# Storing weight differences ahead: the first difference pinned on VectorE, its load two units earlier

## The chip, the cores and the metric

One core of a Trainium2 chip runs the whole kernel. TensorE (PE) multiplies, with its weight loads (PEld) beside it; ACT (ScalarE) and DVE (VectorE) do element-wise work; POOL (GpSimd) here issues the stores and small copies; SP (SyncE) issues the loads. The metric is the device time of one execution in microseconds. The kernel before took 1654.93 us (median of 3 runs, 1653.99 to 1656.75).

## The reference

One decoder layer on 256 tokens of width 2048, in float32:

```
proj = x @ w_in                     # GLA q,k,v,gate,low-rank; FoX q,k,v,forget; two merge gates
o    = gla_chunked(q, k, v, log_a)  # 4 heads, then RMSNorm and swish gate
of   = fox_attention(...)           # 8 heads, causal softmax with forget bias
mix  = (sigmoid(ma)*(o @ w_branch_gla) + sigmoid(mb)*(of @ w_branch_fox)) @ w_out
x    = layer_norm(ALPHA*x + mix)
g    = causal_dwconv(x @ w_gate, conv_w, conv_b)
x    = layer_norm(ALPHA*x + (gelu(g) * (x @ w_up)) @ w_down)
x    = x + sigmoid(x @ w_ple_gate) * (p @ w_ple_proj)
```

Nearly all the work is the products of 256 tokens with large weight matrices, each weight read once.

## The kernel before

**Units.** The weights come in 284 units of 128 x 2048 floats (1 MB), in the order in which they are used (`wu`). Each is loaded by SP in two halves into `raw` (a ring of five buffers). To keep float32 accuracy each half is split: ACT rounds it to `hi` (L120), DVE subtracts to get `lo` (L233), and PE multiplies with both (L299, L301). `hi` and `lo` have six buffers each, three units. `unit()` hands out the next unit and first prepares those up to three ahead, so loads and splits run ahead of PE.

**Stages.** After a start with the FoX values (to about 51 us) come FoX q/k (16 units), GLA q/k (16), the first twenty merge gates, GLA values and gate (32), the other merge gates, the branch projections (24), the output projection (16), gate and up of the MLP (88), down (44) and the last gate (16). Each unit of the first stages ends in an eviction of its PSUM bank: ACT copies half into `tmp`, DVE adds (`comb`, L320 to L330). Small work is woven in by generators: `mixers` (FoX attention and others) and `levels` (the masks and decays of GLA, whose DVE steps `e`, `kq`, `at` alternate with small PE products `pa`).

**Strassen units and stored units.** Some units of the GLA value and gate, output, down and last stages are multiplied by Strassen's scheme in seven products; their four blocks of 512 columns have to be replaced by four differences. Most such units do this when they are prepared. Thirty-one of them do it long before, in stages where there is room ("parked" in the code): `park_gen` loads the unit into a buffer of the S8 pool (`td`), DVE makes the four differences in place (`differences`, L155 to L163, the subtraction on L158), POOL stores the result to a DRAM tensor (L174), and `prep_s` later loads it back (L188). Fifteen of them belong to the GLA value and gate stages and are stored during FoX q/k, GLA q/k and the first merge gates; five belong to the output projection and are stored during the branch projections; eleven belong to down and are stored during gate and up. `park_gen` is a generator: one pull issues the load, the next the four differences and the store.

**The S8 pool** has fifteen buffers of 8 KB a partition. Activations (`xT`, `x1T`, four each), `gq`, `gk`, `gb`, `kq`, `at`, the merge gates `sg`, the hidden activations `hC` (ten of them by the end of gate and up) and the stored units all live there. A load into it waits until the buffer's last user is done.

**What sets the order.** SP's queue is in program order (`manual_schedule`): a load that waits holds back all loads behind it. The other engines' instructions are put in order when the program is built, by a planner with its own costs and the program order as priority; on the chip each engine then goes through its list in that order. `tc.keep_in_program_order(i)` forbids the planner to place an instruction ahead of the one traced just before it on the same engine.

Of the kernel before, what the change touches and what calls it, by code (L numbers as in the profile page):

```python
# [19 lines left out]
P = 128  # L20
# [3 lines left out]
NF = DFF // P  # L24
# [53 lines left out]
def tile_block(ctx: ExitStack, tc: tile.TileContext, wu, wfv, wpp, xT_in, x_in, pT_in, wlr,  # L78
               chan, gnorm, lng, ident_in, mask_in, cmask_in, out):
    nc = tc.nc  # L80
# [23 lines left out]
    def s8(shape, dt=F32, name=None):  # L104
        return big.tile(shape, dt, tag="S8", name=name)

    def t1(name):
        return sm.tile([P, 256], F32, tag="t1", bufs=6, name=name)
# [20 lines left out]
    for _ in range(8):  # L129
# [5 lines left out]
    dn0 = NU - 16 - NF  # L135
# [7 lines left out]
    parked = {b + nh * len(order[nh]) + order[nh].index(n): None  # L143
              for b, order, tset in ((52, GV_ORDER, GV_T), (68, GV_ORDER, GR_T), (120, OUT_ORDER, WO_T),
                                     (dn0, DN_ORDER, DN_T))
              for nh in range(2) for n in tset[nh]}
    parked = {u: i for i, u in enumerate(sorted(parked))}
    td = dr.tile([len(parked), P, 2048], F32, name="td")
# [4 lines left out]
        o = 0 if any(u in r for r in UA) else LO_SHIFT  # L153
        return rlo.tile([P, 1152], F32R, tag="lo", name=f"lo{name}")[:, o:o + 1024]

    def differences(r0, r1, h):
        b12, b11, b22, b21 = r0[:, 0:512], r0[:, 512:1024], r1[:, 0:512], r1[:, 512:1024]
        sub = lambda o, a, b: nc.vector.tensor_tensor(o, a, b, ALU.subtract)  # L158
        if h == 0:
            sub(b11, b12, b11)  # L160
            sub(b12, b12, b22)
        else:
            sub(b22, b22, b11)  # L163
            sub(b21, b21, b22)

    def park_gen(units):

        for u, i in [(u, i) for u, i in parked.items() if u in units]:
            w = s8([P, 2048], name=f"td{i}")
            nc.sync.dma_start(w, wu[u])  # L170
            yield
            for h in range(2):
                differences(w[:, 0:1024], w[:, 1024:2048], h)
            nc.gpsimd.dma_start(td[i], w)  # L174
            yield

    def prep_s(u):

# [33 lines left out]
        if u not in parked:  # L212
            differences(r0, r1, 0)
        t3, t1_ = split(rt[0], "t13")
        if u not in parked:
            differences(r0, r1, 1)
# [24 lines left out]
    def unit(ahead=3):  # L241
        u = n_used[0]
        n_used[0] += 1
        while n_prep[0] < min(NU, u + ahead):
            prep()
        return ready.pop(u)
# [36 lines left out]
    def load_consts2():  # L283
        nc.sync.dma_start(gnb, gnorm.broadcast_to([P, 512]))
        for i in range(2):
            maskf = ring.tile([P, 4, 256], F32, tag="raw", bufs=5, name=f"maskf{i}")
            nc.sync.dma_start(maskf, mask_in[:, 8 * i:8 * i + 8, :].rearrange(
                "p (l t) n -> p l (t n)", t=2))
            nc.gpsimd.tensor_copy(mask[:, 4 * i:4 * i + 4, :], maskf)


    def w_unit(ps, hi, lo, act, kts, first, last, hoff=0, tick=None):


        n = len(kts)
        for i, kt in enumerate(kts):
            a = act[kt // 4]
            w0 = (hoff + i) * P
            nc.tensor.matmul(ps, lhsT=hi[i // 8 if hoff == 0 else 0][:, w0 % 1024:w0 % 1024 + P],  # L299
                             rhs=a[:, kt % 4, :], start=first and i == 0, stop=False)  # L300
            nc.tensor.matmul(ps[:, 256:512],  # L301
                             lhsT=lo[i // 8 if hoff == 0 else 0][:, w0 % 1024:w0 % 1024 + P],
                             rhs=a[:, kt % 4, 0:256], start=False, stop=last and i == n - 1)
            if tick is not None:
                tick(i)
# [15 lines left out]
    def comb(ps, o, scale=1.0):  # L321
        tmp = t1("tmp")
        copy(tmp, ps[:, 256:512], scale)
        a = ps[:, 0:256]
        if len(o.shape) == 3:
            a, tmp = [v.rearrange("p (t n) -> p t n", t=2) for v in (a, tmp)]
        if scale == 1.0:
            nc.vector.tensor_tensor(o, a, tmp, ALU.add)
        else:
            nc.vector.scalar_tensor_tensor(o, a, scale, tmp, ALU.mult, ALU.add)  # L330
# [19 lines left out]
    def pull(n, gens=mixers):  # L350
        for _ in range(n):
            while gens:
                try:
                    next(gens[0])
                    break
                except StopIteration:
                    gens.pop(0)
# [92 lines left out]
    for u in range(8):  # L450
        hi, lo = fvu[u]
        for j in range(2):
# [8 lines left out]
            for t, i, c in seq:  # L461
                o, n = fch[c]
                w, x = prods[t][i]
# [34 lines left out]
    for t in range(2):  # L498
        for c, (o, n) in enumerate(fch):
            n = min(n, 1024 - o)  # L500
# [136 lines left out]


    fqk = {}
    parks = [park_gen(range(52, 84))]  # L640
    load_consts2()
    mixers.append(fox_gen())
    for n in range(16):
        h, j = n // 2, n % 2
        hi, lo = unit()

        ps = (mxtile if n == 0 else mmtile)(f"psf{'qk'[j]}{h}")
        w_unit(ps, hi, lo, xT, range(16), True, True,
               tick=lambda i: pull(1) if i == 7 else None)
        if n % 8 == 0:  # L650
            fqk[h // 4] = s8([P, 4, 2, 256], name=f"fqk{h // 4}")
        comb(ps, fqk[h // 4][:, h % 4, j], (P ** -0.5, 1.0)[j])
        if 8 <= n < 15:
            pull(1, parks)
    tc.keep_in_program_order(nc.scalar.preload_act_table_set("exp_and_others"))

# [10 lines left out]
    def a_gen():  # L667
# [70 lines left out]
        for h in range(H):  # L738
# [8 lines left out]
            for lev in (1, 3, 5, 7):  # L747
                level_put(h, lev)
                if lev < 7:
# [2 lines left out]
                    level(h, lev + 3)  # L752
                    yield

    gq, gk = [s8([P, H, 512], name=n) for n in ("gq", "gk")]
    levels.append(a_gen())


    for n in range(16):
        nm, dst, sc = (("q", gq, 1.0 / 16.0), ("k", gk, 1.0))[n // 2 % 2]  # L760
        h, c = n // 4, n % 2
# [145 lines left out]
    def x_sums(pairs):  # L907
        for i, pair in pairs:
            if i == 0:
                o = s8([P, 8, 256], F32R, name="xS")  # L910
            if i < 2:
                ws = [o[:, 4 * i:4 * i + 4, :]]
            elif i == 3:
                w = ec.tile([P, 2, 512], F32R, tag="vh", name="xS3")
                ws = [w.rearrange("p j (i n) -> p (j i) n", i=2)]
            else:
                ws = [sm.tile([P, 2, 256], F32R, tag="t2", bufs=6, name=f"xS{i}{j}")
                      for j in range(2 if i == 2 else 1)]
                if i == 4:
                    w = ec.tile([P, 512], F32R, tag="vl", name="xS4")  # L920
                    ws.append(w.rearrange("p (i n) -> p i n", i=2))
            m = 4 // len(ws)
            xS[pair] = [ws[j // m][:, j % m, :] for j in range(4)]
            y = t2("xy").rearrange("p (k t) -> p k t", t=S)
            nc.sync.dma_start(y, xT_in[:, 2 * pair:2 * pair + 2, :])
            v = s_sums(y)
            for j, w in enumerate(ws):
                src = v[:, j * m:j * m + m]
                copy(w[:, :, 0:P], src)
                nc.vector.tensor_tensor(w[:, :, P:256], src, w[:, :, 0:P].bitcast(F32),  # L930
                                        ALU.subtract)
            yield
# [15 lines left out]
    def merge_gate(n, tick=None):  # L948
        hi, lo = unit()
        ps = mmtile(f"psm{n}")  # L950
        w_unit(ps, hi, lo, xT, range(16), True, True, tick=tick)
        if n % 8 == 0:
            sg[n // 8] = s8([P, 8, 256], name=f"sg{n // 8}")
        dst = sg[n // 8][:, n % 8, :]
        comb(ps, dst)
        nc.scalar.activation(dst, dst, AF.Tanh, bias=0.0, scale=0.5)

    for n in range(PSM1):
        if 3 <= n < 18:
            pull(1, parks)  # L960
        if n == PSM1 - 6:
            mixers.append(x_sums(list(enumerate(X_S))[:3]))

        merge_gate(n, lambda i: pull(1, levels) if (16 * n + i) * 25 // (16 * PSM1)
                   != (16 * n + i + 1) * 25 // (16 * PSM1) else None)
        pull(1)
# [109 lines left out]
    for n in range(PSM1, 32):  # L1076
        if n in (26, 28):
            i = n // 2 - 13
# [8 lines left out]

    mC, mS = {}, {}
    fhl = None
    parks = [park_gen(range(120, 136))]  # L1090
    for n in range(16):
        hi, lo = unit()
        psa = mmtile(f"psa{n}")
# [25 lines left out]
        i = WO_C.index(pair)  # L1119
# [228 lines left out]
    tc.keep_in_program_order(nc.scalar.preload_act_table_set("gelu_apprx_tanh_and_others"))  # L1348
    late.tile([P, GAPS[2]], F32, name="gap2")
    hC = {}  # L1350
    parks = [park_gen(range(dn0, dn0 + NF))]
    n0 = 6

    def gate_up(name):
# [7 lines left out]
    for n in range(NF):  # L1362
# [18 lines left out]
        u = t1("up")  # L1381
# [4 lines left out]
        if pair in DN_S[0]:  # L1386
            if j == 0:
                yp = t2("yp").rearrange("p (k t) -> p k t", t=S)
            h = yp[:, j, :]
        else:  # L1390
            h = y
# [4 lines left out]
        if pair in DN_S[0] and j == 1:  # L1396
            v = s_sums(yp)
            for i in range(2):
                w = sm.tile([P, 2, 256], F32R, tag="t2", bufs=6, name="hs")
# [291 lines left out]
```

## Time and profile before

| | us |
|---|---|
| median of 3 runs | 1654.93 |
| the profiled execution | 1654.67 |
| its span, first to last instruction | 1652.9 |
| PE busy | 1644.5 |
| PE weight loads busy | 1427.2 |
| DVE busy | 1349.4 |
| ACT busy | 916.5 |

The granted clock was 0.999 of full speed over the span. Busy shares are averages over stages with different limits; a wait counts only if PE in the end waits too. A row of instructions in order of time gives start, duration, engine, line, operation, tile written and tiles read, count, and in brackets how long the engine was idle before it and who released it.

### The profile page before, as it was taken

The numbers are of one execution on the slowest core, as the hardware profiler recorded it, in microseconds if no ns is written. First come the engines' busy times: TensorE is split into PE (matmuls) and PEld (weight loads), VectorE is DVE, ScalarE is ACT, GpSimd is POOL, SyncE is SP. The second block draws the span as 40 slices with busy tenths as digits, with TensorE's granted clock in tenths as the row PEclk, the third lists the DMA queues.
The fourth block names the chain that finished last, engine by engine and source line by source line (L and its number), as shares of the span: only waits on it lengthen the run. The fifth ranks groups of instructions, "written<-read, shape, count | busy, mean of one in ns | idle before, by whom it ended". The sixth has DMA issues, their size and how long they took to land.

```text
span 1652.9 us, 24378 instructions
## 1 busy us (share of the span) xinstructions
PE 1644.5 (99%) x8851; PEld 1427.2 (86%) x8851; DVE 1349.4 (82%) x1988; ACT 916.5 (55%) x1332; POOL 83.1 (5%) x232
## 2 busy tenths in 40 slices
PE   9999999999999999999999999999999999999998
PEld 9988888888888888888898888888888888888887
DVE  7668878998888767978987887787877788988887
ACT  6645545656656654545575455455554556556553
POOL 0000000000000000000010101111101000000000
PEclk9999999999999999999999999999999999999999
DMA  9769688978877657878856787777776779899564
GB/s 323 255 207 357 209 299 292 349 280 304 300 276 268 208 199 273 295 256 295 306 179 203 273 311 254 259 268 273 253 275 239 266 265 339 305 336 337 183 226 127
DMA packets 109512, 442.99 MB, mean 268 GB/s; under 512 B 12440, under 2 KB 13728, under 8 KB 94416
## 3 DMA queue, kind: packets, MB, share of 16 engines
q1 hardware_dynamic: 101616, 395.29, 68.6%
q0 software_dynamic: 7776, 46.15, 7.4%
q8 instruction: 69, 1.13, 0.3%
q14 instruction: 51, 0.42, 0.1%
HBM read 395.24 MB, written 46.15 MB: 267 GB/s over the span
## 4 chain that ended last, share of the span: by engine, by line
PE 92%; DVE 4%; DMA 3%; ACT 1%; issue 1%; SPq 0%; POOL 0%; ACTq 0%; DVEq 0%; POOLq 0%
PE psu L299 10%; PE psg L299 9%; PE dn L830 9%; PE psm L299 5%; PE psu L301 5%; PE psg L301 5%; PE wo L830 4%; PE psa L299 4%; PE gr L830 3%; PE gv L830 3%; PE dn_p L830 3%; PE psm L301 3%; PE pg L345 3%; PE fv L464 2%; PE psa L301 2%; PE psfk L299 2%
## 5 line engine op out<-in xcount | busy, mean ns | idle before, releaser
L233 DVE TENSOR_TENSOR lo<-raw,hi 128x1024 fp32r<-128x1024 f32 x470 | 569.4, 1219 | 133.4 <-ACT hi L120 131.3
L120 ACT ACTIVATE hi<-raw 128x1024 fp32r<-128x1024 f32 x470 | 492.7, 1057 | 309.2 <-issue 109.6
L299 PE MATMUL psu<-x1T,hi 128*128 128x512 f32 x688 | 240.5, 392 | 0.0
L299 PE MATMUL psg<-x1T,hi 128*128 128x512 f32 x672 | 234.9, 392 | 0.0
L301 PE MATMUL psu<-x1T,lo 128*128 128x256 f32 x688 | 192.4, 280 | 0.0
L301 PE MATMUL psg<-x1T,lo 128*128 128x256 f32 x672 | 187.9, 280 | 0.0
L299 PE MATMUL psm<-xT,hi 128*128 128x512 f32 x512 | 180.0, 395 | 0.0
L299 PEld LDWEIGHTS psu<-x1T,hi 128*128 128x128 f32 x688 | 129.2, 188 | 27.6
L299 PEld LDWEIGHTS psg<-x1T,hi 128*128 128x128 f32 x672 | 126.2, 188 | 26.9
L301 PE MATMUL psm<-xT,lo 128*128 128x256 f32 x512 | 143.3, 280 | 0.0
L301 PEld LDWEIGHTS psu<-x1T,lo 128*128 128x128 f32 x688 | 130.6, 190 | 0.0
L301 PEld LDWEIGHTS psg<-x1T,lo 128*128 128x128 f32 x672 | 127.6, 190 | 0.0
L120 ACT ACTIVATE hi_b<-raw 128x512 fp32r<-128x512 f32 x98 | 81.8, 841 | 72.1 <-DMA raw<-in_wu_dram 26.0
L207 DVE TENSOR_TENSOR lo_b<-raw,hi_b 128x512 fp32r<-128x512 f32 x98 | 92.7, 953 | 31.3 <-ACT hi_b L120 31.2
L158 DVE TENSOR_TENSOR td<-td 128x512 f32<-128x512 f32 x124 | 84.9, 684 | 37.4 <-DMA td<-in_wu_dram 36.6
L299 PEld LDWEIGHTS psm<-xT,hi 128*128 128x128 f32 x512 | 96.2, 188 | 20.0
L830 PE MATMUL dn<-hi,hC 128*128 128x512 f32 x352 | 98.0, 389 | 0.0
L301 PEld LDWEIGHTS psm<-xT,lo 128*128 128x128 f32 x512 | 97.2, 190 | 0.2
L299 PE MATMUL psa<-oT,hi 128*128 128x512 f32 x256 | 89.5, 392 | 0.0
L830 PEld LDWEIGHTS dn<-hi,hC 128*128 128x128 f32 x352 | 66.0, 188 | 13.7
L207 DVE TENSOR_TENSOR lo_t<-td,hi_t 128x1024 fp32r<-128x1024 f32 x62 | 73.3, 1218 | 5.0 <-ACT hi_t L120 4.2
L120 ACT ACTIVATE hi_t<-td 128x1024 fp32r<-128x1024 f32 x62 | 64.2, 1054 | 15.8 <-DMA td<-td 10.7
(406 smaller groups left out, 3259.5 us busy)
## 6 DMA issues: line engine op xcount, KB each, us to landing
raw<-in_wu_dram SPq DMA_DIRECT2D x537, 512.0 KB, 5.7
td<-in_wu_dram SPq DMA_DIRECT2D x31, 1024.0 KB, 8.5
td<-td POOLq DMA_DIRECT2D x31, 1024.0 KB, 7.2
td<-td SPq DMA_DIRECT2D x31, 1024.0 KB, 7.7
hS<-sd SPq DMA_DIRECT2D x11, 1024.0 KB, 8.4
raw<-in_wu_dram SPq DMA_DIRECT2D x31, 256.0 KB, 7.2
fvraw<-in_wfv_dram SPq DMA_DIRECT2D x13, 524.0 KB, 7.0
sd<-hs POOLq DMA_DIRECT2D x24, 256.0 KB, 6.2
```

The costliest lines, as they stand in the source:

```text
L120: return nc.scalar.activation(o, i, AF.Copy, bias=0.0, scale=scale)
L158: sub = lambda o, a, b: nc.vector.tensor_tensor(o, a, b, ALU.subtract)
L207: nc.vector.tensor_tensor(lo, src, hi.bitcast(F32), ALU.subtract)
L233: i = nc.vector.tensor_tensor(lo, raw, hi.bitcast(F32), ALU.subtract)
L299: nc.tensor.matmul(ps, lhsT=hi[i // 8 if hoff == 0 else 0][:, w0 % 1024:w0 % 1024 + P], rhs=a[:, kt % 4, :], start=first and i == 0, stop= ...
L301: nc.tensor.matmul(ps[:, 256:512], lhsT=lo[i // 8 if hoff == 0 else 0][:, w0 % 1024:w0 % 1024 + P], rhs=a[:, kt % 4, 0:256], start=False, ...
L345: nc.tensor.matmul(bs[j][:, 0:m], lhsT=x, rhs=v[:, o:o + m], start=first and i == 0, stop=last and i == 2)
L464: nc.tensor.matmul(fbk[t][c][:, 0:n], lhsT=x, rhs=w[:, o:o + n], start=kt == 0 and i == 0, stop=kt == 15 and i == 2)
L830: nc.tensor.matmul(ps[:, e], lhsT=x, rhs=w, start=todo[id(ps)] == total[id(ps)], stop=todo[id(ps)] == 1)
```

## The change

The four differences and the store move into a function `park`; the first difference is kept in program order on DVE. `park_gen` takes two numbers, `lag` (pulls from the load to `park`) and `rest` (pulls from `park` to the next load). The kernel before had one pull for each. The stored units are the same and are read back at the same places.

| stage | loads before | stores before | loads after | stores after |
|---|---|---|---|---|
| FoX q/k, iterations | 8, 10, 12, 14 | 9, 11, 13 | 4, 7, 10, 13 | 6, 9, 12, 15 |
| GLA q/k, iterations | 9, 11, 13, 15 | 8, 10, 12, 14 | 8, 10, 12, 14 | 10, 12, 14 |
| first merge gates, passes | 4, 6, ... 16 | 3, 5, ... 17 | 0, 2, ... 12 | 0, 2, ... 14 |
| branch projections, gate and up | as pulled, one pull apart | | the same pulls | the same pulls |

In the first two stages the pull comes at the end of an iteration, in the merge gates at the beginning of a pass.

```diff
-    def differences(r0, r1, h):
+    def differences(r0, r1, h, pinned=False):
...
         if h == 0:
-            sub(b11, b12, b11)
+            i = sub(b11, b12, b11)
+            if pinned:
+                tc.keep_in_program_order(i)
             sub(b12, b12, b22)
...
-    def park_gen(units):
+    def park(w, i):
+        for h in range(2):
+            differences(w[:, 0:1024], w[:, 1024:2048], h, h == 0)
+        nc.gpsimd.dma_start(td[i], w)
 
-        for u, i in [(u, i) for u, i in parked.items() if u in units]:
-            w = s8([P, 2048], name=f"td{i}")
+    def park_gen(units, lag, rest):
+        for u in units:
+            w = s8([P, 2048], name=f"td{parked[u]}")
             nc.sync.dma_start(w, wu[u])
-            yield
-            for h in range(2):
-                differences(w[:, 0:1024], w[:, 1024:2048], h)
-            nc.gpsimd.dma_start(td[i], w)
-            yield
+            for _ in range(lag):
+                yield
+            park(w, parked[u])
+            for _ in range(rest):
+                yield
...
-    parks = [park_gen(range(52, 84))]
+    stored = [u for u in parked if 52 <= u < 84]
+    parks = [park_gen(stored[:4], 2, 1)]
...
-        if 8 <= n < 15:
+        if n >= 4:
             pull(1, parks)
...
+    parks = [park_gen(stored[4:8], 2, 0), park_gen(stored[8:], 2, 0)]
     gq, gk = [s8([P, H, 512], name=n) for n in ("gq", "gk")]
...
     for n in range(PSM1):
-        if 3 <= n < 18:
-            pull(1, parks)
+        pull(1, parks)
...
-    parks = [park_gen(range(120, 136))]
+    parks = [park_gen([u for u in parked if 120 <= u < 136], 1, 1)]
...
-    parks = [park_gen(range(dn0, dn0 + NF))]
+    parks = [park_gen([u for u in parked if dn0 <= u < dn0 + NF], 1, 1)]
```

## The prediction

> **What bounds the kernel now.** I read the head of the page and the shares of the chain first, because they say which engine sets the end.
>
> ```profile
> span 1652.9 us, 24378 instructions
> PE 1644.5 (99%) x8851; PEld 1427.2 (86%) x8851; DVE 1349.4 (82%) x1988; ACT 916.5 (55%) x1332; POOL 83.1 (5%) x232
> PE 92%; DVE 4%; DMA 3%; ACT 1%; issue 1%; SPq 0%; POOL 0%; ACTq 0%; DVEq 0%; POOLq 0%
> ```
>
> TensorE is busy for all but 8.4 us of the span, so the question for any edit is which of TensorE's waits it removes or makes. The chain gives 7% to VectorE and DMA. Its longest pieces that are not TensorE, in the stretch where fifteen units are stored, are three loads of such units:
>
> ```profile
> 223.56 8.74 DMA td<-in_wu_dram
> 259.24 8.34 DMA td<-in_wu_dram
> 273.30 8.96 DMA td<-in_wu_dram
> ```
>
> Next come the waits: VectorE's on these loads over the whole run (total, times, longest), then those of TensorE's weight loads between 140 and 380 us (all of them), and the one matmul behind the longest of these.
>
> ```profile
> DVE td L158 <- DMA td<-in_wu_dram: 36.6, 12, 5.3
> PEld pa L685 <- DVE phl L679: 0.8, 2, 0.5
> PEld pa L726 <- DVE kq L709: 0.8, 1, 0.8
> PEld pa L726 <- DVE kq L719: 0.3, 1, 0.3
> 273.62 0.49 PE L726 MATMUL pa<-kq 128*128 128x128 f32 x2 [0.60 <-DVE kq L709]
> ```
>
> The reader is to see a filter. VectorE stands idle 36.6 us for loads of stored units, because the planner put the first difference ahead of other work and the load landed later than it thought. Of this, only 1.9 us come through to TensorE (0.8 + 0.8 + 0.3), all at the small GLA matmuls that read what VectorE had just made. The rest is swallowed by weights split ahead. The stretches show the same:
>
> ```profile
> 225.00:250.00 25.00, 24.66 (x145) 21.74 (x145) 20.36 (x35) 11.25 (x22) 0.53 (x1) 1.00 0.88 320
> 250.00:275.00 25.00, 24.39 (x149) 21.70 (x148) 20.74 (x36) 12.01 (x21) 0.53 (x1) 1.00 0.75 258
> 275.00:300.00 25.00, 24.90 (x150) 22.00 (x149) 23.63 (x40) 15.71 (x30) 1.06 (x2) 1.00 0.97 350
> 300.00:325.00 25.00, 25.00 (x152) 22.29 (x151) 24.83 (x46) 14.05 (x23) 1.06 (x2) 1.00 0.93 332
> 325.00:350.00 25.00, 25.00 (x152) 22.32 (x151) 23.57 (x46) 13.87 (x29) 1.07 (x2) 1.00 1.00 383
> ```
>
> The columns are the stretch and its length, then busy time and count of PE, PEld, DVE, ACT and POOL, then clock, DMA share and GB/s. TensorE lacks 0.34, 0.61 and 0.10 us in the first three and nothing in the next two, though VectorE is busiest there (24.83 of 25).
>
> **The change part by part.** Durations come from this execution; it took 1654.67 us, 1.8 us more than its span, and the median of the runs shown, 1654.93, is 0.26 us above that.
>
> ```profile
> L158 DVE TENSOR_TENSOR td<-td x124: 665/683/695, 107.3 to 1285.9; 128x512 f32<-128x512 f32 x124
> L233 DVE TENSOR_TENSOR lo<-raw,hi 128x1024 fp32r<-128x1024 f32 x470 | 569.4, 1219 | 133.4 <-ACT hi L120 131.3
> td<-in_wu_dram SPq DMA_DIRECT2D x31, 1024.0 KB, 8.5
> td<-td POOLq DMA_DIRECT2D x31, 1024.0 KB, 7.2
> raw<-in_wu_dram SPq DMA_DIRECT2D x537, 512.0 KB, 5.7
> 1227.14 0.39 PE L299 MATMUL psg<-x1T,hi 128*128 128x512 f32 x1
> 1260.42 0.39 PE L299 MATMUL psg<-x1T,hi 128*128 128x512 f32 x1
> ```
>
> The last two rows start iterations 35 and 38 of gate/up (the code's two units each): 33.28 us for six units, 5.55 us a unit.
>
> *What stays.* 31 loads, 124 differences of 683 ns and 31 stores stay, 1 MB a transfer; VectorE's busy time and the traffic do not change. Work: 0 us.
>
> *The pin.* The first difference of each unit may no longer go ahead of the last VectorE instruction traced before it: in the FoX, GLA and merge stretches the add that evicts a unit from PSUM, in the later ones the last step of that iteration. The other three follow it by their data. What is queued behind it is that engine's later splits and GLA levels. With two units (11.1 us) between load and difference, on top of SP running ahead of TensorE, a load of 8.5 us has landed; in the later stages one pull lies between. So of the 36.6 us nearly all should go. On the path this is worth at least the 0.60 us that the matmul row shows and at most the 1.9 us of the weight loads. I take 1.5: the three stretches lack 0.34 + 0.61 + 0.10 = 1.05 us of modelled matmul time, and a modelled end hides part of a wait. What is late next: the four differences now stand together, 4 x 0.683 = 2.7 us, behind an eviction and ahead of the next GLA step. A delay of 2.7 us is shorter than the 8.74, 8.34 and 8.96 us pieces that cost 1.9 us together, 0.6 each. Scaled by length that is 0.2 us a place; over eleven places between 0 and 2.2 us. I take 0.2 in all, since VectorE, no longer stopped, stands further ahead of TensorE.
>
> *The places in FoX.* Loads move from iterations 8, 10, 12, 14 to 4, 7, 10, 13, and all four stores are out by iteration 15. The cover is the split weights: one place where they are short before is this, in order of issue (ACT evicts, ACT splits the next unit only then; TensorE's unit that needs it two later).
>
> ```profile
> 112.00 0.38 ACT L120 ACTIVATE tmp<-psfk 128x256 f32<-128x256 f32 x1 [5.16 <-PE psfk L301]
> 112.28 1.05 ACT L120 ACTIVATE hi<-raw 128x1024 fp32r<-128x1024 f32 x1
> 118.99 0.39 PE L299 MATMUL psfk<-xT,hi 128*128 128x512 f32 x1
> ```
>
> ACT idled 5.16 us there with the split placed behind the eviction. In the code the old load of iteration 8 follows at once the first use of a new S8 buffer (`fqk1`); the new ones do not. I read this as the planner holding SP's later loads back in its plan. TensorE did not wait there, so removing it is worth 0.
>
> *GLA and merge gates.* Loads move one iteration earlier in GLA (8, 10, 12, 14), and in the merge gates to the top of passes 0, 2, ... 12, the last store at 14 where it was 17. A store and the next load come in one pull. SP meets that load some units before the store; it needs a free S8 buffer then. Counting live ones (four `xT`, `gb`, `kq`, `at`, `gq`, `gk`, two `sg`) leaves four of fifteen; a stored unit holds one for about five units at one per two units, some 2.7. SP is not held: 0 us, bounded above by rival A's price.
>
> *Later stages.* Positions stay; only the pin is new. In the branch projections about three buffers are free: 0 us. At the end of gate/up four `x1T` and ten `hC` leave one. There each load waits for the store of the unit before:
>
> ```profile
> 1232.77 0.42 SPq L170 DMA_DIRECT2D td<-in_wu_dram  x1
> 1272.00 0.48 SPq L170 DMA_DIRECT2D td<-in_wu_dram  x1
> 1218.69 0.54 POOL L174 DMA_DIRECT2D td<-td  x1 [4.92 <-DVE td L158]
> 1260.86 0.54 POOL L174 DMA_DIRECT2D td<-td  x1 [4.19 <-DVE td L158]
> 1232.28 0.42 DVE L1395 TENSOR_TENSOR hC<-yp,hC 128x256 fp32r<-128x256 f32 x1
> 1269.67 0.43 DVE L1401 TENSOR_TENSOR hs<-sums,hs 128x256 fp32r<-128x256 f32 x1 [1.03 <-ACT hs L120]
> 1293.70 0.39 PE L299 MATMUL psg<-x1T,hi 128*128 128x512 f32 x1
> ```
>
> The last three stored units are loaded in iterations 33, 36, 39 and differenced in 34, 37, 40. Iteration 34 ends at 1227.14 and its last VectorE step at 1232.7, so the pinned differences end at 1235.4 or at 1238, if they spread over some 5 us (the store before waited 4.92 us for them); the store lands 7.2 us later, by 1243 to 1245. The next load, wanted at 1232.77, is held 10 to 12 us. Behind it in SP's queue stand the raw loads of the unit that TensorE starts at 1260.42: 1245 + 5.7 + 1.05 (split on ACT) + 1.22 (VectorE) = 1253, 7 us early. Iteration 37 ends its last step at 1270.1; store out by 1273 to 1275, landed by 1280 to 1282; the load of 1272.00 is held 8 to 10 us, and the raws for 1293.70 come to 1282 + 8.0 = 1290, 3.7 us early. They run beside a 1 MB load on that queue, which can eat the 3.7. I take 0 here, between 0 and 3 (an eviction at 1293.7 first, then 0.38 + 1.05 + 1.22).
>
> **Sum.** 1654.67 - 1.5 + 0.2 + 0 = 1653.4 for the profiled execution, and 0.26 above for the median: 1653.6. With all bounds met at once the execution would take 1654.67 - 1.9 = 1652.8 or 1654.67 - 0.6 + 2.2 + 3 = 1659.3.
>
> **The rivals.** *A, the late buffer* (slower or even). The held load at 1272.00 empties SP's lead and TensorE waits at 1293.7, up to 3 us; it decides once the store lands 3.7 us after my 1282. Speaks for it: one buffer, the pin on the last step of an iteration. Against: 8 to 10 us of hold out of the 21.7 from 1272.00 to 1293.70. Time 1654.7 to 1656.6.
>
> *B, a split one unit too late* (slower). The planner sets ACT's splits behind an eviction where its own plan sees the raw load late. Before this comes within a hair of TensorE:
>
> ```profile
> 1055.26 0.43 SPq L170 DMA_DIRECT2D td<-in_wu_dram  x1
> 1077.58 0.38 ACT L120 ACTIVATE tmp<-psg 128x256 f32<-128x256 f32 x1 [3.73 <-PE psg L301]
> 1077.86 1.05 ACT L120 ACTIVATE hi<-raw 128x1024 fp32r<-128x1024 f32 x1
> 1081.25 1.22 DVE L233 TENSOR_TENSOR lo<-raw,hi 128x1024 fp32r<-128x1024 f32 x1
> 1082.92 0.39 PE L299 MATMUL psg<-x1T,hi 128*128 128x512 f32 x1
> ```
>
> The low half is ready at 1082.5, and the unit that needs it starts at 1082.92. One eviction later, TensorE would stand still for a unit, from 1077.58 to 1082.92 = 5.3 us or so. One such place decides: 1653.6 + 5.3 = 1658.9. For: the pin changes the plan everywhere, and it makes buffers come free later in the plan too. Against: three of the four differences interleaved here (about 2 us) go to a later place, and new loads avoid fresh S8 buffers in FoX.
>
> *C, no effect.* If the differences already come late enough or other stops replace them, 1654.9. Against: twelve waits of up to 5.3 us on loads cannot stand with two units between.
>
> *D, much more to gain.* If 36.6 us of VectorE idleness slowed TensorE unseen, more than 3.3 us could go, below 1651.6. The Trainium skill, "Trainium Kernel Development and Optimization", section Performance Expectations, says that matmul busy time is a bad measure of the distance to the limit and weight-load busy time a good one. By that rule 86% would leave 14%, some 225 us, open in a kernel such as this, and the 99% would mean little. Here the rows decide the chance: in 300 to 350 no weight load waits and PEld still reads 22.3 of 25, so 89% is packed here, and the three poorer stretches lack 0.56 + 0.60 + 0.30 = 1.5 us against that. The same 1.5, not 30.
>
> **How the numbers follow.** Forecast 0.60 (1652.9 to 1654.6), C 0.07, A 0.15, B 0.14, D 0.04. The shown runs spread by 2.8 us, so about 0.2% or 3.3 us is what a measurement can tell from no change. Only D lies beyond it below: faster 0.04. B lies beyond it above, and a bad A with something beside it: slower 0.16. The rest, 0.80, is within. The range runs from 1652.0, a little under all 1.9 us gained, to 1657.0, above A; it leaves out D and most of B.
>
> **What would show it.** Right: no row of VectorE waiting on the loads of stored units, or a few us; no such load in the chain between 220 and 290; the `pa` waits of TensorE gone or under 0.5 us; four stores before 165 us; VectorE's busy time near 1349. At the end of gate/up the last two loads come near 1244 and 1281. Wrong: a TensorE wait of over 1 us on a low half `lo`, above all near 1083, 1260 or 1294, or `pa` waits that stay though the loads no longer hold VectorE.

## The result and the profile after

The changed kernel took 1654.05 us (median of 21 runs, 1653.36 to 1656.14). The kernel before, run beside it, took 1657.18 us (median of 21, 1653.02 to 1660.3). The ratio is 0.9982 with a 95% interval of 0.9975 to 0.9988: 3.1 us faster. The median of 1654.93 that stood in the section on time and profile came from three of these 21, all below the median of the 21.

The profiled execution took 1653.9 us, with a span of 1651.7. Against the execution profiled before, the span is 1.2 us shorter and the time 0.8 us. The 0.4 us between lies outside the span and belongs to the program: it is 2.2 us in each run of the changed kernel and 1.8 us in each run of the one before.

First the head of the page and the shares of the chain, of the kernel after:

```profile
span 1651.7 us, 24375 instructions
PE 1644.2 (100%) x8851; PEld 1427.0 (86%) x8851; DVE 1353.7 (82%) x1988; ACT 917.4 (56%) x1332; POOL 83.5 (5%) x232
PE 96%; DVE 2%; ACT 1%; DMA 1%; issue 0%; POOL 0%; ACTq 0%; DVEq 0%
```

VectorE has as much to do as before (1353.7 us, 1349.4 before), but its share of the chain falls from 4% to 2%, and that of DMA from 3% to 1%. The next two views are VectorE's two longest rows of waits over the whole run, total first, and the only wait listed of TensorE's weight loads between 140 and 380 us:

```profile
DVE lo L240 <- ACT hi L120: 155.8, 174, 3.3
DVE lo_b L214 <- ACT hi_b L120: 34.8, 28, 4.2
```

```profile
PEld pa L734 <- DVE kq L717: 0.2, 1, 0.2
```

The row of 36.6 us, waits on the loads of stored units, is gone, and the chain between 220 and 290 us holds TensorE alone, no load. Of the 1.9 us of waits at `pa`, 0.2 us is left. The stretches that lacked time, with the same columns as before:

```profile
225.00:250.00 25.00, 25.00 (x150) 22.22 (x149) 23.14 (x38) 14.43 (x26) 0.59 (x2) 1.00 0.97 372
250.00:275.00 25.00, 25.00 (x155) 22.40 (x154) 22.96 (x42) 12.72 (x22) 1.54 (x3) 1.00 0.98 353
275.00:300.00 25.00, 25.00 (x152) 22.32 (x152) 24.84 (x41) 14.75 (x28) 1.07 (x2) 1.00 0.95 335
```

TensorE is full in all three (24.66, 24.39 and 24.90 before). VectorE does 2 to 3 us more work in the first two and 1.2 us more in the third, and TensorE loses nothing by it.

### The profile page after: what moved, and what is told of

The parts are those of the page before. It is cut to its first block, busy times and chain, and to the rows that moved or that the text cites. A ratio compares the mean times of both kernels' runs of the same rounds, so it can differ in the third digit from the quotient of the medians.

```text
span 1651.7 us, 24375 instructions
## 1 busy us (share of the span) xinstructions
PE 1644.2 (100%) x8851; PEld 1427.0 (86%) x8851; DVE 1353.7 (82%) x1988; ACT 917.4 (56%) x1332; POOL 83.5 (5%) x232
## 4 chain that ended last, share of the span: by engine, by line
PE 96%; DVE 2%; ACT 1%; DMA 1%; issue 0%; POOL 0%; ACTq 0%; DVEq 0%
PE psu L306 10%; PE psg L306 9%; PE dn L839 9%; PE psm L306 7%; PE psu L308 5%; PE psg L308 5%; PE wo L839 4%; PE psa L306 4%; PE gr L839 3%; PE psm L308 3%; PE gv L839 3%; PE dn_p L839 3%; PE fv L471 3%; PE pg L352 3%; PE psa L308 2%; PE psk L306 2%
## 5 line engine op out<-in xcount | busy, mean ns | idle before, releaser
L839 PEld LDWEIGHTS dn<-hi,hC 128*128 128x128 f32 x352 | 66.0, 188 | 13.7
```

The lines of the kernel that those rows point to most:

```text
L839: nc.tensor.matmul(ps[:, e], lhsT=x, rhs=w, start=todo[id(ps)] == total[id(ps)], stop=todo[id(ps)] == 1)
```

## The experiments

All ratios are to the kernel before, run beside the experiment. The experiments were timed in three groups, and the medians of the kernel before in them were 1657.41, 1657.56 and 1656.86 us. Where a span is given, it is that of the profiled execution.

### Which part does it: the pin or the places

The change has two parts: the pin of the first difference on VectorE, for all 31 stored units, and new places of load and difference for the first fifteen. Four kernels take them apart. The first is the kernel before with the pin alone:

```diff
+            i = sub(b11, b12, b11)
+            if pinned:
+                tc.keep_in_program_order(i)
...
-                differences(w[:, 0:1024], w[:, 1024:2048], h)
+                differences(w[:, 0:1024], w[:, 1024:2048], h, h == 0)
```

> The kernel before with nothing but the pin on the first difference of all 31 stored units; loads and stores stay at their old pulls. Theory 'pin' (VectorE's stops for late loads cost the time, and cost more in the runs that the first profile did not show): ratio to the kernel before 0.9982 +- 0.0006 as the whole change, 36.6 us of VectorE waits on these loads down to under 5 us, the waits of the small GLA products 'pa' under 0.5 us. Theory 'places' (the new pulls matter): ratio 1.000 +- 0.0005. Theory of the fresh buffer in FoX: the split behind the eviction near 112 us stays here, because the load still follows the first use of a new buffer in iteration 8.

It took 1654.07 us, ratio 0.9982 (0.9973 to 0.9991): the whole gain. VectorE waits on no stored load any more, and one `pa` wait of 0.5 us is left. With the old places, the split behind an eviction near 112 us stays too. Rows of ScalarE:

```profile
112.08 0.38 ACT L120 ACTIVATE tmp<-psfk 128x256 f32<-128x256 f32 x1 [5.16 <-PE psfk L303]
112.36 2.00 ACT L120 ACTIVATE hi<-raw 128x1024 fp32r<-128x1024 f32 x2
```

The second is the changed kernel without the pin:

```diff
-            differences(w[:, 0:1024], w[:, 1024:2048], h, h == 0)
+            differences(w[:, 0:1024], w[:, 1024:2048], h, False)
```

> The changed kernel without the pin: new pulls, two units between load and difference in program order, but the planner is free to move the first difference forward. Theory 'pin': VectorE's waits on these loads come back (20 to 40 us) and the ratio is 0.999 to 1.000. Theory 'places': 0.9982 as the whole change, waits under 5 us. Fresh buffer: the split behind the eviction near 112 us is gone.

It took 1653.15 us, ratio 0.9976 (0.9967 to 0.9985): the whole gain again, where the theory that the pin is what pays had expected next to none. The waits of its VectorE, first over the whole run and then between 140 and 380 us:

```profile
DVE td L158 <- DMA td<-in_wu_dram: 24.4, 12, 4.4
```

```profile
DVE td L158 <- DMA td<-in_wu_dram: 1.5, 2, 1.1
```

So either part suffices for the first fifteen: the pin keeps the difference from being put ahead of its data, and two units between load and difference leave the load time to land wherever the planner puts the difference. Each of the two theories was half wrong: 24.4 us of the waits came back, and the gain stayed all the same. Outside this window 22.9 us of VectorE's waits stay, and they cost nothing that the time shows. The third and fourth kernels split the pin by stage: the changed kernel with the pin on the first fifteen units alone, and the kernel before with the pin on the other sixteen alone.

```diff
-            differences(w[:, 0:1024], w[:, 1024:2048], h, h == 0)
+            differences(w[:, 0:1024], w[:, 1024:2048], h, pinned and h == 0)
...
-            park(w, parked[u])
+            park(w, parked[u], u < 84)
```

> Pin and new pulls for the fifteen units stored before 375 us; the sixteen later ones (branch projections, gate and up) as before, without the pin. Theory 'early' (only waits behind the small GLA products reach TensorE): the whole gain, ratio 0.9982 +- 0.0006. Rival 'late' (the two places near 1083 and 1260 us, where the low half is ready less than 1 us ahead in the profile of before, become waits in other runs): 0.9995 to 1.000, and with spread runs as before.

```diff
-                differences(w[:, 0:1024], w[:, 1024:2048], h)
+                differences(w[:, 0:1024], w[:, 1024:2048], h, h == 0 and u >= 84)
```

> The complement: old pulls and no pin for the fifteen early units, the pin for the sixteen later ones. Theory 'early': 0.9995 to 1.000, 'pa' waits of 1 to 2 us stay. Rival 'late': 0.9982 to 0.999, runs close together. If both halves count, this ratio and that of the early half multiply to 0.9982.

The former took 1653.36 us, ratio 0.9979 (0.997 to 0.9988), with 18.4 us of waits on stored loads left in the later stages. The latter took 1658.12 us, ratio 1.0005 (0.9996 to 1.0014): no gain. Its waits between 140 and 380 us:

```profile
PEld pa L687 <- DVE phl L681: 1.0, 2, 0.7
PEld pa L728 <- DVE kq L711: 0.9, 1, 0.9
PEld pa L728 <- DVE kq L721: 0.2, 1, 0.2
```

The gain comes from the first fifteen units, and the pin in the later stages is worth nothing. VectorE waits on stored loads as long in the one place as in the other (16.1 us between 140 and 380 us here, 18.4 us in the later stages above), but only the former come with waits of TensorE at `pa`, the small products that read what VectorE has just made.

### Which units

The next two put the pin, with the lines shown first, into the kernel before: on stored units 4 to 9 alone (the GLA stage and the first merge gates), and on the other 25 alone:

```diff
+                differences(w[:, 0:1024], w[:, 1024:2048], h, h == 0 and 4 <= i < 10)
```

> The kernel before with the pin on the six stored units 4 to 9 alone, those for whose loads VectorE stopped in the early stages; all pulls old. Theory 'early, through VectorE's stops': whole gain, ratio 0.9982 +- 0.0008, runs within 3 us of each other. Rival 'order' (the pin helps because the plan of everything else changes, or through the FoX units): less than half, 0.999 to 1.000.

```diff
+                differences(w[:, 0:1024], w[:, 1024:2048], h, h == 0 and not 4 <= i < 10)
```

> The complement: the pin on the other 25 stored units, 4 to 9 free. Theory 'early, through VectorE's stops': no gain, 0.9995 to 1.0005, 'pa' waits 1.5 to 2.5 us, runs spread over 5 us. Rival 'order': 0.9982 to 0.999.

The first took 1653.82 us, ratio 0.9979 (0.9971 to 0.9988); the second 1656.29 us, ratio 0.9996 (0.9988 to 1.0005). What the second leaves, by the waits of TensorE's weight loads and of VectorE between 140 and 380 us:

```profile
PEld pa L728 <- DVE kq L711: 1.5, 1, 1.5
PEld pa L687 <- DVE phl L681: 0.9, 2, 0.6
PEld pa L687 <- ACT phl L120: 0.7, 1, 0.7
```

```profile
DVE td L158 <- DMA td<-in_wu_dram: 14.4, 5, 6.0
```

With a fourth row of 0.2 us these are 3.3 us at `pa`, more than the 1.5 to 2.5 expected. As far as the intervals tell, six units hold the whole gain. Two of them were tried alone, 5 and 6, whose differences are the first of VectorE's long stops:

```diff
+                differences(w[:, 0:1024], w[:, 1024:2048], h, h == 0 and i in (5, 6))
```

> The kernel before with the pin on stored units 5 and 6 alone, the two whose loads stop VectorE between 207 and 235 us. In the slower execution profiled, TensorE waited 1.5 and 1.0 us at 239 to 242 behind them, and then ran 3.3 us at half clock. Theory 'waits and the clock after them': the wait at 239 goes, those near 273 and 289 stay; over half of the gain, ratio 0.9983 to 0.9990, and runs closer together than before. Rival (each of the six counts alike, no part for the clock): a third, 0.9993.

It took 1653.5 us, ratio 0.9983 (0.9973 to 0.9992), and the waits between 140 and 380 us shrank to these:

```profile
PEld pa L728 <- DVE kq L721: 0.2, 1, 0.2
```

```profile
DVE td L158 <- DMA td<-in_wu_dram: 2.1, 1, 2.1
```

The pin on two of 31 differences brings the gain. The expectation that the waits near 273 and 289 us would stay was wrong: the stops hang together. One link can be VectorE's own backlog, as it is busy for 20 to 25 of each 25 us from 225 us on. The other link is SP's queue. A `raw` buffer comes free when VectorE has split it, so a VectorE that stands still holds SP's raw loads and, behind them, the next stored load. SP's waits for VectorE's splits between 209 and 224 us (total, times, longest), first in the kernel before, then here:

```profile
SPq L229 <- DVE lo L233: 13.8, 4, 8.6
```

```profile
SPq L231 <- DVE lo L235: 7.3, 4, 2.4
```

The loads of units 6, 8 and 9 were issued at 223.56, 259.24 and 273.30 us in the kernel before, and at 217.93, 253.30 and 266.25 us here. Of VectorE's five stops between 140 and 380 us, 15.8 us in all, one of 2.1 us is left, at unit 4. So each `pa` wait read alone looked like a matter of the load just before it, and they had a common start. How much each link carries was not tested apart, and the planner also put the differences of units 7 and 8 in somewhat other places.

### What the longer executions of the kernel before hold

The prediction's 1.9 us of `pa` waits came from an execution of 1654.67 us, and the median of 21 runs was 1657.18. The kernel before, unchanged, was profiled twice more.

> The kernel before, unchanged, for a second profile of it. Both theories need to know what lies in its slower executions (to 1661 us, where the profile shown took 1654.67). Theory 'early': where this execution takes longer than 1655.5, the excess stands as longer 'pa' waits of TensorE between 190 and 300 us, behind longer stops of VectorE for loads of stored units (over 15.7 us there). Rival 'elsewhere': the 'pa' waits stay at 1.9 us and the excess is in another stage.

This execution took 1657.48 us with a span of 1655.7. Its waits of TensorE's weight loads between 140 and 380 us, VectorE's waits on stored loads over the whole run, and two pieces of the chain:

```profile
PEld pa L685 <- ACT phl L120: 1.8, 1, 1.8
PEld pa L685 <- DVE phl L679: 1.2, 1, 1.2
PEld pa L726 <- DVE kq L719: 0.2, 1, 0.2
```

```profile
DVE td L158 <- DMA td<-in_wu_dram: 38.5, 12, 6.0
```

```profile
208.88 10.71 DMA td<-in_wu_dram
225.44 9.53 DMA td<-in_wu_dram
```

These are the loads of units 5 and 6; in the first profile the same two took 10.1 and 8.7 us. VectorE's stop at unit 5 grew from 5.1 to 6.0 us, its stops between 140 and 380 us from 15.8 to 18.6 us, and the waits at `pa` from 1.9 to 3.2 us. Something else follows them, which was not expected. Rows of TensorE, then two stretches (25 us, and the one of the slow matmuls):

```profile
238.16 0.39 PE L299 MATMUL psk<-xT,hi 128*128 128x512 f32 x1
238.51 0.39 PE L299 MATMUL psk<-xT,hi 128*128 128x512 f32 x1
...
239.43 0.28 PE L301 MATMUL psk<-xT,lo 128*128 128x256 f32 x1
241.18 0.38 PE L685 MATMUL pa<-phl,ones 128*128 128x256 f32 x1 [1.47 <-ACT phl L120]
242.53 0.39 PE L685 MATMUL pa<-phl,ones 128*128 128x256 f32 x1 [0.97 <-DVE phl L679]
...
243.51 0.63 PE L299 MATMUL psk<-xT,hi 128*128 128x512 f32 x1
244.15 0.63 PE L299 MATMUL psk<-xT,hi 128*128 128x512 f32 x1
...
246.71 0.44 PE L299 MATMUL psk<-xT,hi 128*128 128x512 f32 x1
```

```profile
225.00:250.00 25.00, 22.56 (x123) 19.56 (x122) 19.58 (x35) 10.16 (x19) 0.53 (x1) 0.93 0.87 304
243.40:246.70 3.30, 3.30 (x12) 2.83 (x11) 3.30 (x8) 2.52 (x7) 0.00 (x0) 0.50 0.98 293
```

TensorE waits 1.47 and 0.97 us with one small matmul between. Less than a microsecond after the second the granted clock falls to 0.50, for about 3.4 us: over the microsecond from 243 us it reads 0.69, over that from 246 us 0.61. In this time a pair of `hi` and `lo` matmuls takes 0.64 us from start to start instead of the 0.35 of the first two rows; five pairs from 243.51 to 246.71 cost 3.20 - 5 x 0.35 = 1.45 us. None of that is a wait, so no list of waits has it. In the 25 us TensorE's busy time is short by 2.44 us, and these 1.45 come on top.

> A third profile of the kernel before. Theory 'waits and the clock after them': its span above 1650.9 is the sum of its 'pa' waits in 190 to 300 us and of half the time at half clock there, plus up to 1 us of waits of the start and the down stage. Where the granted clock stays full after the waits, it takes under 1656 us.

The third execution took 1656.48 us, with a span of 1654.7 and the clock full. The expectation that it would be below 1656 with a full clock failed by 0.5 us. Its waits between 140 and 380 us, then two rows of the list over the whole run:

```profile
PEld pa L726 <- DVE kq L709: 1.3, 1, 1.3
PEld pa L685 <- DVE phl L679: 0.7, 2, 0.4
...
PEld pa L685 <- ACT phl L120: 0.2, 1, 0.2
```

```profile
PEld fv L464 <- ACT fvhi L120: 1.5, 3, 0.7
...
PEld dn_p L830 <- DVE lo_t L207: 1.2, 3, 0.6
```

Waits of 1.3 us left the clock alone. The rest of its excess over the first execution lies at the start, which takes 0.4 us longer, and in the down stage, 0.9 us longer, where these two rows stand. The change touches neither.

The mean granted clock of every timed run says how often the drop happens. Half clock for 3.4 us takes 0.001 off the mean of a 1655-us span. Of the 90 timed runs of the kernel before in the three groups, 24 had a mean clock of 0.998 or 0.997, with a median time of 1658.7; the 66 others had 1656.9. Of the 32 timed runs of the changed kernel (21 and 11) none had less than 0.999. So the executions with a lower clock account for some 24/90 x 1.8 = 0.5 us of the gain, the waits that go with the fall included, and 2.9 us (1656.9 to 1654.05) remain where the clock is full. Where in those runs the clock fell isn't known, since only the one has a trace. Nor does the size of the wait alone decide: the kernel with the other 25 units pinned kept waits of 0.6 to 1.5 us and had no low clock in 11 runs, and the one with the later sixteen pinned had it in 4 of 11.

The sum over profiles: the spans of the kernel before were 1652.9, 1655.7 and 1654.7, mean 1654.4; those of the changed kernel 1651.7 and 1651.4, mean 1651.55 (the second profile stands with the next experiments). Of the difference of 2.9 us, the `pa` waits account for (1.9 + 3.2 + 2.4)/3 - 0.2 = 2.3 and the half clock for 1.45/3 = 0.5. That closes it for the profiled executions.

The time between two fixed matmuls of TensorE shows the same without any list of waits. From the first `psq` matmul to the first `psa` matmul, which are GLA q/k to the end of the other merge gates, the three executions of the kernel before took 462.6, 465.3 and 463.1 us, and both of the changed kernel 460.7 us. The differences of 1.9, 4.6 and 2.4 us are, to within 0.2 us, the `pa` waits of the weight loads, in the second execution with the 1.45 us of half clock. In the experiments the stretch took 461.0 us (pin alone), 460.3 (places alone), 461.4 (units 4 to 9) and 460.8 (units 5 and 6), against 462.8 (later sixteen) and 464.0 (other 25). The gain lies in this stretch.

Over the timed runs the median spans differ by 3.7 us (1655.5 over the 90, 1651.8 over the 21), and 0.4 of it is given back outside the span; about 0.9 us of the 3.7 has no row of its own.

### The loads that follow a fresh buffer, and a better version

The prediction read the split behind the eviction near 112 us as caused by a load traced just behind the first use of a new S8 buffer, and saw another split behind an eviction, with less room, near 1083 us (rival B). In the kernel with the new places alone, where FoX's loads no longer follow `fqk1`, the split stands ahead of that eviction:

```profile
112.09 1.06 ACT L120 ACTIVATE hi<-raw 128x1024 fp32r<-128x1024 f32 x1 [1.71 <-PE psfk L306]
113.05 0.37 ACT L120 ACTIVATE tmp<-psfk 128x256 f32<-128x256 f32 x1
```

Gate and up has two loads traced that way, in iterations 20 and 36. One more kernel has the new places, no pin, and these two loads in iterations 21 and 35:

```diff
-            differences(w[:, 0:1024], w[:, 1024:2048], h, h == 0)
+            differences(w[:, 0:1024], w[:, 1024:2048], h, False)
...
-        if n >= n0 and (n - n0) * steps // (NF - 3 - n0) != (n - n0 + 1) * steps // (NF - 3 - n0):
+        if n in GU:
```

with `GU = (7, 9, 10, 11, 13, 15, 17, 19, 21, 22, 23, 25, 26, 27, 29, 31, 33, 34, 35, 36, 38, 40)`.

> The new pulls without the pin, and in gate and up the loads moved off the iterations that first use a new buffer for the hidden activations: none in iteration 20 or 36, but in 21 and 35. Reading of the fresh buffer: the low halves for the units near 1081 and 1259 us, ready 0.7 us ahead with the loads in 20 and 36, are ready 8 us ahead or more; other reading (the planner's place of the differences does it): still under 3 us. Either way TensorE did not wait there, so the ratio stays at that of the new pulls alone, 0.9976 +- 0.0008; if the slower executions came from these two places it would fall further, to 0.997.

It took 1653.15 us, ratio 0.9974 (0.9965 to 0.9983). The split for the unit that starts at 1081 is now made 13.7 us ahead of its matmuls, where the changed kernel (its rows stand further down) and the kernel with the new places alone make it 5.1 us ahead. Rows of ScalarE and TensorE:

```profile
1067.28 1.06 ACT L120 ACTIVATE hi<-raw 128x1024 fp32r<-128x1024 f32 x1 [1.44 <-issue]
...
1081.02 0.39 PE L306 MATMUL psg<-x1T,hi 128*128 128x512 f32 x1
```

The low half is ready 11.1 us ahead, and that of the unit at 1258.51 10.4 us ahead; with the new places alone both are ready 0.45 us ahead. So the reading of the cause holds in gate and up, where only the two loads were moved, and FoX, where all four were, agrees: take the load away from the new buffer and the late split goes. But the median is the same 1653.15 as with the new places alone: the lead of under a microsecond was thin and cost nothing. Beside each other, the changed kernel and this one:

> The changed kernel itself, beside the next one on one chip: 0.9982 +- 0.0006 to the kernel before.

> The new pulls without the pin, gate and up loads off the fresh buffers, beside the changed kernel. If not pinning is really better by the 0.9 us of the medians so far, its median lies 0.5 to 1.3 us under that of the changed kernel here too; if that was chance, within 0.4 us.

The changed kernel took 1653.95 us (ratio 0.9987, 0.9978 to 0.9996) and the other one 1652.99 us (ratio 0.9978, 0.9969 to 0.9987). The difference of the medians is 0.96 us, as the first of the two readings expected. The intervals of the two ratios overlap, but 11 of the 12 runs without the pin lie below the changed kernel's median. Half of the difference lies outside the span (2.2 us against 1.8), the other half in the spans (medians 1651.7 and 1651.2). Here the changed kernel's profile has two small waits, of which the other one's keeps part of the first and nothing of the second:

```profile
PEld go L1041 <- DVE oT L1078: 0.8, 2, 0.5
PEld dn_p L839 <- DVE lo_t L214: 0.6, 1, 0.6
```

```profile
PEld go L1041 <- DVE oT L1078: 0.3, 1, 0.3
```

Only the first is a matter of the kernel: it is 0.3 us in all three profiles of the new places without the pin, and 0.8 us in both of the changed kernel. The second is 0.6 us in the other profile of this same program (1653.15 us), so it comes and goes. The program has the lowest median of those that were run, by a small margin.

## Why the prediction was right, and where its size was off

The forecast was 1653.6 us, between 1652.0 and 1657.0, and 1654.05 us was measured. The mechanism was right too: VectorE's stops for the loads go, and with them the waits at `pa`. One term was mis-sized. By its steps:

*The pin, "nearly all should go".* Right: 36.6 us to no row at all. *"At least the 0.60 us ... at most the 1.9 us ... I take 1.5."* This is the mis-sized term. In the profiled executions 1.9 - 0.2 = 1.7 us of `pa` waits went; over the three profiles of before it is 2.3, and with the lower clock and the rest it is 3.1 us of time. The lower bound also left out a second wait of a `pa` matmul, of 0.3 us at L685. The bounds came from one execution near the lower end of the kernel's spread (1654.67 in 1653.02 to 1660.3). The stops of VectorE change between executions: between 140 and 380 us they were 15.8, 16.4 and 18.6 us in the three profiles, and the `pa` waits 1.9, 2.4 and 3.2 us, so about half of what the stops grew by came through. It was luck that the forecast came so near the measured time, because it started from a median 2.25 us below that of 21 runs: 1653.6 stands 3.6 below 1657.18, not the 1.3 that was worked out.

*The bound by modelled matmul time.* "The three stretches lack 1.05 us" was used to pull 1.9 down to 1.5. It was the wrong step: from the first `psq` to the first `psa` matmul the execution after is 1.9 us shorter, which is all that the weight loads had waited. Its span is only 1.2 us shorter because the start and the down stage took 0.2 and 0.5 us longer. These differ by as much between the two executions of the changed kernel, 0.3 and 0.5 us.

*The four differences together, 0.2 us (0 to 2.2).* Right at its lower end: one `pa` wait of 0.2 us is left, with VectorE at 24.84 of 25 us. *The same work.* Right: 1353.7 against 1349.4.

*FoX, worth 0.* Right. The eviction's split behind a late load went with the new places and stayed with the old ones, and the two kernels' times do not show it. That the first four stores came before 165 us is no test: the change has the last of them at 157.26 us, but the kernel before had it earlier, at 146.12.

*What the prediction didn't ask* is whether pin and places are both needed. It booked the whole gain under the pin, with the two units between load and difference as part of the reason, and the places in GLA and the merge gates at 0. Either does it alone.

*Rival A, the late buffer.* It didn't come. The two last loads in SP's queue, then the low halves made after the second and the matmuls of the unit in question:

```profile
1239.44 0.33 SPq L177 DMA_DIRECT2D td<-in_wu_dram  x1
1278.15 0.33 SPq L177 DMA_DIRECT2D td<-in_wu_dram  x1
```

```profile
1286.22 3.82 DVE L240 TENSOR_TENSOR lo<-raw,hi 128x1024 fp32r<-128x1024 f32 x3 [2.88 <-ACT hi L120]
1291.96 0.39 PE L306 MATMUL psg<-x1T,hi 128*128 128x512 f32 x1
```

The loads are held as forecast, to 1239.44 and 1278.15, where 1243 to 1245 and 1280 to 1282 were forecast on a timeline that lies 1.7 us later (1293.70 against 1291.96): 2 to 4 us and up to 2 us sooner than worked out. The first of the three low halves is the one that the unit at 1291.96 needs. It is ready at 1286.22 + 1.22 = 1287.44, 4.5 us ahead (forecast 3.7).

*Rival B, a split one unit too late.* It didn't come, and the place moved the other way. ScalarE's, VectorE's and TensorE's rows near 1083:

```profile
1076.12 1.05 ACT L120 ACTIVATE hi<-raw 128x1024 fp32r<-128x1024 f32 x1
...
1078.23 1.22 DVE L240 TENSOR_TENSOR lo<-raw,hi 128x1024 fp32r<-128x1024 f32 x1
...
1081.19 0.39 PE L306 MATMUL psg<-x1T,hi 128*128 128x512 f32 x1
```

The low half is ready at 1079.45, 1.7 us ahead of the matmuls, where the kernel before had 0.4. *Rival C, no effect*, fell with the ratio's interval. *Rival D, much more to gain*, fell too: the three stretches now read 22.22, 22.40 and 22.32 of 25 us for weight loads with hardly a wait, as the packed stretches did before, and the time stayed above 1651.6.

## What to carry to other kernels

An engine's idle time on a load counts only where another engine is about to read what stands behind it, so follow the wait to the first reader: here the pin on 2 of 31 differences brought the whole gain, and 22.9 us of the same waits in other stages cost nothing. An engine that stops on a load can also stop freeing buffers: here the next stored loads came 6 to 7 us later, and further stops with them. So test by removing the first stops, not the one next to the late reader. Before the size of such a wait is taken from one profile, place that execution in the spread of the runs: the delay varies, part of what it grows by comes through, and a quick execution shows little of it.

## What the runs showed of the hardware

The granted clock of TensorE fell to 0.50 for about 3.4 us after waits of 1.47 and 0.97 us with one small matmul between, and five pairs of matmuls took 0.64 instead of 0.35 us each. A stall of 2.4 us thus cost 1.45 us more after it had ended. The Trainium skill, "TensorE: Matmul & The Clock Gate", section "Part 1: The HAM clock gate (the "warmup" mystery)", says that the clock is halved after at least one idle window of about 3.4 us and comes back after a busy one. The return after about 3.4 us agrees with it; the fall did not need a full window of idleness here, as TensorE did a matmul between the two waits and stood still for 2.4 us in all.

In the first execution of the kernel before, the 31 loads of 1 MB took from 6.7 to 10.9 us from issue to landing. One and the same load, that of unit 5, took 10.1, 10.7 and 9.6 us in three executions. And the time outside the span differs by program and hardly between runs: 1.8 us before, 2.2 after, medians of 1.76 to 2.23 among the others. Nothing in the traces tells what it is.
